# Splitting weights by pairs of k-tiles in the first layer and the attention values, and sharing the split pool with the MLPs

## The chip, the cores and the metric

The kernel runs on one core of one Trainium2 chip. The metric is the time of one execution on the device, in microseconds (us). Engines are named as in the profile: PE multiplies matrices (PEld loads its weights), DVE, ACT and POOL work on vectors, SP issues the DMA transfers from its queue.

## What is computed

Two layers over 256 positions of width 2048, all float32, here in short form. The first is an RWKV-7 time mixing, the second an attention with forget gates over shared keys and values; each is followed by an MLP with squared ReLU of width 8192.

```python
rkv = jnp.einsum('bsnd,nde->bsne', xs[:, :, :3], w_rkv)      # three 2048x2048 projections
y = rwkv7_recurrence(rh, dh, kh, vh, -kk, kk * ah)
x = x + (y * g) @ w_o
x = x + jnp.square(jax.nn.relu(rms_norm(x) @ w_up[0])) @ w_down[0]
k, v, f = split(rms_norm(x) @ w_kvf)                         # keys, values, forget gates
x = x + attention(rms_norm(x) @ fox_w_q, k, v, cumsum(log_sigmoid(f))) @ fox_w_o
x = x + jnp.square(jax.nn.relu(rms_norm(x) @ w_up[1])) @ w_down[1]
out = rms_norm(x)
```

Gains, mixing with the previous position, the low-rank gates and softmax are left out of this extract.

## The kernel before

PE multiplies float32 through operands that are rounded for it (`F32R`). To keep precision every weight is split in two: a high part `wh`, the rounded copy, and a low part `wl`, what the rounding dropped. A product then takes a matmul of the high part with each part of the activations, and one of the low part with their high part. `load_split` does it: a DMA from SP's queue brings a raw tile `wr` (512 KB), ACT casts it to `wh` (L203) and DVE subtracts to get `wl` (L205). A raw tile is free when its last subtraction has ended; a split tile when PE's last matmul with it has.

A raw tile of the first layer holds two k-tiles of 128 rows, 512 columns each. `per` says how many k-tiles go into one split. Before, the first layer (`gemm_steps` for w_rkv and w_o, `gv` for the first layer's values), the attention's keys (`wide_sums` with `per` 1) and its values split one k-tile at a time, 128x512; `narrow_steps`, for the queries and fox_o, takes four k-tiles of 256 columns by twos, 128x512 as well. The MLPs split two k-tiles at once, 128x1024.

The raw tiles of all stages come from the pool `wraw` (4 buffers). The splits outside the MLPs come from `wsp` (5 buffers each of `wh` and `wl`, 128x512), those of the MLPs from a pool `ms` of their own (`WSP`, 4 buffers of 128x1024).

The stages follow one another, with some overlap: the first layer's projections beside the preparation of the recurrence (to about 330 us of the span), the recurrence (to 620), the tail of w_o, the first MLP (660 to 1357), keys and values (to 1540), queries, heads and fox_o (to 1780), and the second MLP. Inside the first layer two plans, written as tables of numbers, mix the streams: `gk`, `gr` and `gv` are the groups of columns of the three projections, `prep` makes the recurrence's operands (kk, bk, ksq and others on DVE; stores to and loads from scratch memory `s_e`, `s_at`, `s_k`, `s_b` through SP). In the second plan every eighth cast goes to DVE (L201) and every fifth subtraction to POOL; these are counted per split. The order on each engine is set by a scheduler that works with estimated times, and each engine and SP's queue take theirs in that order.

Of the kernel before, what the change touches and what calls it, by code (L numbers as in the profile page):

```python
# [18 lines left out]
P = 128  # L19
# [9 lines left out]
RMS_EPS = 1e-6  # L29
CDEC = math.exp(-0.5)  # L30
NEG = -1.0e30
WK, WSP = 2, 4

VEC = ["mix0", "mix1", "ffn0", "ffn1", "fin", "kvn", "xm0", "xm1", "xm2", "xm3", "xm4", "xm5",
       "w0", "a0", "kk", "ka", "rk", "lnw", "lnb"]
# [83 lines left out]
def trunk_kernel(ctx: ExitStack, tc: tile.TileContext, xin, vecs, bfv, c32, c16, w_rkv, w1, w2, a1, a2, g1, g2,  # L119
# [9 lines left out]
    nc.scalar.preload_act_table_set("natural_log_exp_and_others")  # L129

    cpool = ctx.enter_context(tc.tile_pool(name="const", bufs=1))
    wraw = ctx.enter_context(tc.tile_pool(name="wraw", bufs=4))
    wsp = ctx.enter_context(tc.tile_pool(name="wsp", bufs=5))
    big = ctx.enter_context(tc.tile_pool(name="big", bufs=1))
    psm = ctx.enter_context(tc.tile_pool(name="psm", bufs=4, space=PSUM))
    pss = ctx.enter_context(tc.tile_pool(name="pss", bufs=4, space=PSUM))
# [2 lines left out]
    opA = big.tile([P, KT, 2, T], F32R, name="opA")  # L139
# [50 lines left out]

    share = {"n": 0, "h": 0, "l": 0}

    def load_split(src, p, nk, n, per=1, wraw=wraw, wsp=wsp):
        raw = wraw.tile([p, nk, n], F32, tag="wr", name="wr")
        dma(raw, src)
        hl = []
        for k in range(0, nk, per):
            h = wsp.tile([p, per, n], F32R, tag="wh", name="wh")
            c = share["n"] = share["n"] + 1
            if share["h"] and c % share["h"] == 0:  # L200
                V.tensor_copy(h, raw[:, k:k + per, :])  # L201
            else:
                nc.scalar.copy(h, raw[:, k:k + per, :])  # L203
            lo = wsp.tile([p, per, n], F32R, tag="wl", name="wl")
            (G if share["l"] and c % share["l"] == 0 else V).tensor_tensor(  # L205
                lo, raw[:, k:k + per, :], h.bitcast(F32), op=ALU.subtract)
            hl += [(h[:, i, :], lo[:, i, :]) for i in range(per)]
        return hl
# [6 lines left out]
    def gemm_steps(w, col, xh, xl, evac, ks=None, ps=None, ready=None):  # L215
# [6 lines left out]
        if fresh:  # L222
            ps += [psm.tile([P, 2, T], F32, tag="mm", name="mm") for _ in range(2)]
        for k0 in ks[::2]:
            hl = load_split(w[k0 * P:(k0 + 2) * P, col:col + 512].rearrange("(k p) n -> p k n", p=P), P, 2, 512)
            for kk in range(2):
                k = k0 + kk
                assert ready is None or ready(k)
                h, lo = hl[kk]
                for m in range(4):  # L230
                    mm3(ps[m // 2][:, m % 2, :], h[:, m * P:(m + 1) * P], lo[:, m * P:(m + 1) * P],
                        xh[:, k, :], xl[:, k, :], k == ks[0] and fresh, k == KT - 1, m % 2 == 0)
                yield
# [522 lines left out]
    def gv(g):  # L756

        ps = [psm.tile([P, 512], F32, tag="mm", name="mmv") for _ in range(2)]
        for k0 in range(0, KT, 2):
            hl = load_split(w_rkv[2][k0 * P:(k0 + 2) * P, 512 * g:512 * g + 512].rearrange("(k p) n -> p k n", p=P),  # L760
                            P, 2, 512)
            for kk in range(2):
                k, (h, lo) = k0 + kk, hl[kk]
                assert k < mixed[2]
# [196 lines left out]
    def after0(kp):  # L961
        norm2.add(kp)
        operand("kvn", kp, opBH, opBL)
    with tc.tile_pool(name="msp0", bufs=WSP, reuse_waits="tile") as ms, \
            tc.tile_pool(name="mlp0", bufs=2, reuse_waits="tile") as mp:
        for g in range(4):
            gemm_group(w_o, 512 * g, opAH, opAL, o_evac_for(g), range(12, 16), po[g] if g < 2 else None)
        mlp(0, norm, mp, (wraw, ms), opB, opA, after0)


    s_c = dpool.tile([HEADS, T], F32, name="s_c")
# [1 line left out]
    with tc.tile_pool(name="fox", bufs=2, reuse_waits="tile") as fp:  # L973
# [63 lines left out]
        for g in range(4):  # L1037
            ps = [psm.tile([P, 512], F32, tag="mm", name="mmv") for _ in range(2)]
            for k0 in range(0, KT, 2):
                c = D + 512 * g  # L1040
                hl = load_split(w_kvf[k0 * P:(k0 + 2) * P, c:c + 512].rearrange("(k p) n -> p k n", p=P), P, 2, 512)
                for kk in range(2):
                    k = k0 + kk
                    for i in range(2):
# [94 lines left out]

    norm4 = Norm(npool, "n3")  # L1140
    with tc.tile_pool(name="msp1", bufs=WSP, reuse_waits="tile") as ms, \
            tc.tile_pool(name="mlp1", bufs=2, reuse_waits="tile") as mp:

        def after1(kp):
# [2 lines left out]
                return  # L1147
            for k in range(2 * kp if kp < KT // 2 - 1 else 2 * kp - 2, 2 * kp + 2):
                act(xT[:, k, :], xT[:, k, :], AF.Copy, scale=vcol("fin", k))
        mlp(1, norm3, mp, (wraw, ms), opA, opB, after1)  # L1150
        norm4.ln()

        rp = side("rf")[:, 0:T]
# [61 lines left out]
```

## Time and profile before

| | us |
|---|---|
| median of 3 runs | 2475.38 |
| fastest and slowest run | 2474.15, 2476.15 |
| the profiled execution, its time | 2474.56 |
| its span in the trace | 2472.8 |
| PE busy | 2429.4 (98%) |
| DVE busy | 1513.6 (61%) |
| ACT busy | 1235.7 (50%) |
| POOL busy | 243.8 (10%) |

The profiled execution's time is 1.8 us more than its span, which lies around it, and 0.8 us under the median of the runs. Busy shares are means over the span. A line such as `L205 DVE TENSOR_TENSOR wl<-wr,wh 128x512` is the instruction's source line, its engine, operation, written and read tiles, and the shape for one instruction; what follows `|` is the busy time in us, the mean of one in ns, and the engine's idle time ahead of them with what ended it. A time line has the start, the duration and how many instructions stand in the row. Where instructions overlap, the end of one lies behind the start of the next.

### The profile page before, as it was taken

To read this page: it belongs to the slowest core of one execution; us is meant where nothing else is said; L and a number is where in the kernel's file an instruction comes from. 1 tells how busy PE (TensorE), PEld (TensorE's weight loads), DVE (VectorE), ACT (ScalarE), POOL (GpSimd) and SP (SyncE) were. 2 spreads that over 40 slices of the span, in tenths; PEclk is the share of its full clock that TensorE was granted. 3 is DMA by queue.
4 is the path that set the end of the run, shared out by engine and by line. 5 is a ranking of instruction groups with operands and counts; after the bars stand their busy time and mean duration, and the time that the engine had idled before them with its cause. 6 is when DMAs were issued, how large, how long until landed. Compare 5 with 4: busy or idle time off the path is not lost.

```text
span 2472.8 us, 45748 instructions
## 1 busy us (share of the span) xinstructions
PE 2429.4 (98%) x18336; PEld 2087.4 (84%) x18336; DVE 1513.6 (61%) x2201; ACT 1235.7 (50%) x1969; POOL 243.8 (10%) x241
## 2 busy tenths in 40 slices
PE   8999999999999999999999999999999999999998
PEld 6999877689888888888888888888888888888886
DVE  8986666765854455554557565787654555555554
ACT  3766444454654453453455544565454543443543
POOL 2000112221300010000011000111010000000001
PEclk9999999999999999999999999999999999999999
DMA  5777765564766666666665656545656666666653
GB/s 166 229 248 246 261 196 172 185 189 147 230 190 190 194 187 195 190 187 194 191 184 179 189 178 194 170 158 176 201 182 196 190 188 195 190 189 195 189 186 125
DMA packets 276565, 472.56 MB, mean 191 GB/s; under 512 B 23280, under 2 KB 70656, under 8 KB 276352
## 3 DMA queue, kind: packets, MB, share of 16 engines
q1 hardware_dynamic: 276352, 469.64, 61.2%
q8 instruction: 143, 2.34, 0.4%
q14 instruction: 70, 0.57, 0.1%
HBM read 445.44 MB, written 24.13 MB: 190 GB/s over the span
## 4 chain that ended last, share of the span: by engine, by line
PE 91%; DVE 4%; issue 2%; DMA 1%; ACT 1%; POOL 0%; SPq 0%; POOLq 0%; DVEq 0%; ACTq 0%
PE mmw L253 21%; PE mmw L257 11%; PE mmd L390 9%; PE mmd L389 9%; PE mmd L391 9%; PE mmn L271 5%; PE mm L211 3%; PE mm L212 3%; PE mm L213 3%; PE mmn L275 2%; PE mmv L767 1%; PE i L693 1%; PE mmv L768 1%; PE mmv L769 1%; PE zyus L869 1%
## 5 line engine op out<-in xcount | busy, mean ns | idle before, releaser
L205 DVE TENSOR_TENSOR wl<-wr,wh 128x1024 fp32r<-128x1024 f32 (+1 forms) x1001 | 964.1, 974 | 769.2 <-ACT wh L203 682.8
L203 ACT CAST wh<-wr 128x512 fp32r<-128x512 f32 (+1 forms) x1010 | 839.4, 837 | 976.8 <-PE mmd L390 345.0
L253 PE MATMUL mmw<-opB,wh 128*128 128x512 f32 x1280 | 321.2, 393 | 0.0
L253 PEld LDWEIGHTS mmw<-opB,wh 128*128 128x128 f32 x1280 | 230.4, 189 | 41.7 <-ACT nln L351 0.3
L253 PE MATMUL mmw<-opA,wh 128*128 128x512 f32 x1024 | 256.7, 393 | 0.0
L253 PEld LDWEIGHTS mmw<-opA,wh 128*128 128x128 f32 x1024 | 184.4, 189 | 33.3 <-ACT nln L351 0.3
L389 PE MATMUL mmd<-wh,opB 128*128 128x512 f32 x512 | 199.7, 390 | 0.0
L389 PE MATMUL mmd<-wh,opA 128*128 128x512 f32 x512 | 199.7, 390 | 0.0
L390 PE MATMUL mmd<-wh,opA 128*128 128x512 f32 x512 | 199.3, 389 | 0.0
L391 PE MATMUL mmd<-wl,opA 128*128 128x512 f32 x512 | 199.3, 389 | 0.0
L391 PE MATMUL mmd<-wl,opB 128*128 128x512 f32 x512 | 199.3, 389 | 0.0
L390 PE MATMUL mmd<-wh,opB 128*128 128x512 f32 x512 | 199.3, 389 | 0.0
L419 POOL TENSOR_TENSOR ms<-mt 128x512 f32<-128x512 f32 x64 | 78.5, 1239 | 1157.7 <-ACT mt L417 1157.7
L257 PEld LDWEIGHTS mmw<-opB,wl 128*128 128x128 f32 x1280 | 174.5, 190 | 14.9 <-DVE wl L205 2.6
L257 PE MATMUL mmw<-opB,wl 128*128 128x256 f32 x1280 | 178.7, 283 | 1.8 <-DVE wl L205 1.8
L211 PE MATMUL mm<-opA,wh 128*128 128x256 f32 x512 | 150.5, 294 | 0.0
L257 PEld LDWEIGHTS mmw<-opA,wl 128*128 128x128 f32 x1024 | 139.8, 190 | 10.0
L212 PE MATMUL mm<-opA,wh 128*128 128x256 f32 x512 | 145.5, 284 | 0.0
L213 PE MATMUL mm<-opA,wl 128*128 128x256 f32 x512 | 145.1, 283 | 0.0
L257 PE MATMUL mmw<-opA,wl 128*128 128x256 f32 x1024 | 142.8, 282 | 0.0
L391 PEld LDWEIGHTS mmd<-wl,opB 128*128 128x128 f32 x512 | 96.1, 188 | 20.0
L391 PEld LDWEIGHTS mmd<-wl,opA 128*128 128x128 f32 x512 | 96.1, 188 | 20.0
(293 smaller groups left out, 3833.5 us busy)
## 6 DMA issues: line engine op xcount, KB each, us to landing
wr<-in_mlp_w_up_dram SPq DMA_DIRECT2D x256, 512.0 KB, 3.8
wr<-in_mlp_w_down_dram SPq DMA_DIRECT2D x256, 512.0 KB, 3.7
wr<-in_w_rkv_dram SPq DMA_DIRECT2D x96, 512.0 KB, 5.0
wr<-in_w_kvf_dram SPq DMA_DIRECT2D x64, 512.0 KB, 3.7
wr<-in_w_o_dram SPq DMA_DIRECT2D x32, 512.0 KB, 4.6
wr<-in_fox_w_q_dram SPq DMA_DIRECT2D x32, 512.0 KB, 3.5
wr<-in_fox_w_o_dram SPq DMA_DIRECT2D x32, 512.0 KB, 3.7
wr<-in_g_dram SPq DMA_DIRECT2D x8, 512.0 KB, 4.7
```

The source lines that it names most:

```text
L203: nc.scalar.copy(h, raw[:, k:k + per, :])
L205: (G if share["l"] and c % share["l"] == 0 else V).tensor_tensor(lo, raw[:, k:k + per, :], h.bitcast(F32), op=ALU.subtract)
L211: mm(ps, wh, xh, start=first and bank_first, stop=False, skip_group_check=True)
L212: mm(ps, wh, xl, start=False, stop=False, skip_group_check=True)
L213: mm(ps, wl, xh, start=False, stop=last, skip_group_check=True)
L253: mm(ps[m], h[:, m * P:(m + 1) * P], x[:, k].rearrange("p h t -> p (h t)"), start=k == 0, stop=False, skip_group_check=True)
L257: mm(ps[m][:, 0:T], lo[:, m * P:(m + 1) * P], x[:, k, 0, :], start=False, stop=k == KT - 1, skip_group_check=True)
L271: mm(ps[m], hl[i][0][:, m * P:(m + 1) * P], x[:, k0 + i].rearrange("p h t -> p (h t)"), start=k0 + i == 0, stop=False, skip_group_check=True)
L389: mm(ps[i], b[:, k, 0, t], h, start=k == 0, stop=False)
L390: mm(ps[i], b[:, k, 1, t], h, start=False, stop=False)
L391: mm(ps[i], b[:, k, 0, t], lo, start=False, stop=k == KT - 1)
L419: G.tensor_tensor(s, t, t, op=ALU.mult)
```

## The change

The first layer's three projections and w_o, and the attention's values, now call `load_split` with `per` 2: one cast and one subtraction of 128x1024 for two k-tiles. `wsp` holds 3 buffers instead of 5; a buffer there now is as large as its largest tile, a pair. `wraw` holds 3 instead of 4. Keys, queries and fox_o still split 128x512 tiles, through the same 3 buffers. The MLPs get raw tiles of their own (`mr`, 4 buffers) and take their splits in turn from `wsp` and from `ms`, which has 2 buffers (3 + 2 pairs in rotation). Since the counts of `SHARE_B` run per split, the second plan now has half as many splits, and gives DVE 7 casts and POOL 11 subtractions of 128x1024 where it gave 14 and 23 of 128x512.

```diff
@@ -29,7 +29,7 @@
 RMS_EPS = 1e-6
 CDEC = math.exp(-0.5)
 NEG = -1.0e30
-WK, WSP = 2, 4
+WK, WSP = 2, 2
 
 VEC = ["mix0", "mix1", "ffn0", "ffn1", "fin", "kvn", "xm0", "xm1", "xm2", "xm3", "xm4", "xm5",
        "w0", "a0", "kk", "ka", "rk", "lnw", "lnb"]
@@ -129,8 +129,8 @@
     nc.scalar.preload_act_table_set("natural_log_exp_and_others")
 
     cpool = ctx.enter_context(tc.tile_pool(name="const", bufs=1))
-    wraw = ctx.enter_context(tc.tile_pool(name="wraw", bufs=4))
-    wsp = ctx.enter_context(tc.tile_pool(name="wsp", bufs=5))
+    wraw = ctx.enter_context(tc.tile_pool(name="wraw", bufs=3))
+    wsp = ctx.enter_context(tc.tile_pool(name="wsp", bufs=3))
     big = ctx.enter_context(tc.tile_pool(name="big", bufs=1))
     psm = ctx.enter_context(tc.tile_pool(name="psm", bufs=4, space=PSUM))
     pss = ctx.enter_context(tc.tile_pool(name="pss", bufs=4, space=PSUM))
@@ -190,6 +190,15 @@
 
     share = {"n": 0, "h": 0, "l": 0}
 
+    class Turns:
+
+        def __init__(self, *pools):
+            self.pools, self.n = pools, {}
+
+        def tile(self, shape, dtype, tag, name):
+            n = self.n[tag] = self.n.get(tag, -1) + 1
+            return self.pools[n % len(self.pools)].tile(shape, dtype, tag=tag, name=name)
+
     def load_split(src, p, nk, n, per=1, wraw=wraw, wsp=wsp):
         raw = wraw.tile([p, nk, n], F32, tag="wr", name="wr")
         dma(raw, src)
@@ -222,7 +231,7 @@
         if fresh:
             ps += [psm.tile([P, 2, T], F32, tag="mm", name="mm") for _ in range(2)]
         for k0 in ks[::2]:
-            hl = load_split(w[k0 * P:(k0 + 2) * P, col:col + 512].rearrange("(k p) n -> p k n", p=P), P, 2, 512)
+            hl = load_split(w[k0 * P:(k0 + 2) * P, col:col + 512].rearrange("(k p) n -> p k n", p=P), P, 2, 512, 2)
             for kk in range(2):
                 k = k0 + kk
                 assert ready is None or ready(k)
@@ -758,7 +767,7 @@
         ps = [psm.tile([P, 512], F32, tag="mm", name="mmv") for _ in range(2)]
         for k0 in range(0, KT, 2):
             hl = load_split(w_rkv[2][k0 * P:(k0 + 2) * P, 512 * g:512 * g + 512].rearrange("(k p) n -> p k n", p=P),
-                            P, 2, 512)
+                            P, 2, 512, 2)
             for kk in range(2):
                 k, (h, lo) = k0 + kk, hl[kk]
                 assert k < mixed[2]
@@ -962,10 +971,11 @@
         norm2.add(kp)
         operand("kvn", kp, opBH, opBL)
     with tc.tile_pool(name="msp0", bufs=WSP, reuse_waits="tile") as ms, \
+            tc.tile_pool(name="mraw0", bufs=4, reuse_waits="tile") as mr, \
             tc.tile_pool(name="mlp0", bufs=2, reuse_waits="tile") as mp:
         for g in range(4):
             gemm_group(w_o, 512 * g, opAH, opAL, o_evac_for(g), range(12, 16), po[g] if g < 2 else None)
-        mlp(0, norm, mp, (wraw, ms), opB, opA, after0)
+        mlp(0, norm, mp, (mr, Turns(wsp, ms, wsp, ms, wsp)), opB, opA, after0)
 
 
     s_c = dpool.tile([HEADS, T], F32, name="s_c")
@@ -1038,7 +1048,7 @@
             ps = [psm.tile([P, 512], F32, tag="mm", name="mmv") for _ in range(2)]
             for k0 in range(0, KT, 2):
                 c = D + 512 * g
-                hl = load_split(w_kvf[k0 * P:(k0 + 2) * P, c:c + 512].rearrange("(k p) n -> p k n", p=P), P, 2, 512)
+                hl = load_split(w_kvf[k0 * P:(k0 + 2) * P, c:c + 512].rearrange("(k p) n -> p k n", p=P), P, 2, 512, 2)
                 for kk in range(2):
                     k = k0 + kk
                     for i in range(2):
@@ -1139,6 +1149,7 @@
 
     norm4 = Norm(npool, "n3")
     with tc.tile_pool(name="msp1", bufs=WSP, reuse_waits="tile") as ms, \
+            tc.tile_pool(name="mraw1", bufs=4, reuse_waits="tile") as mr, \
             tc.tile_pool(name="mlp1", bufs=2, reuse_waits="tile") as mp:
 
         def after1(kp):
@@ -1147,7 +1158,7 @@
                 return
             for k in range(2 * kp if kp < KT // 2 - 1 else 2 * kp - 2, 2 * kp + 2):
                 act(xT[:, k, :], xT[:, k, :], AF.Copy, scale=vcol("fin", k))
-        mlp(1, norm3, mp, (wraw, ms), opA, opB, after1)
+        mlp(1, norm3, mp, (mr, Turns(wsp, ms, wsp, ms, wsp)), opA, opB, after1)
         norm4.ln()
 
         rp = side("rf")[:, 0:T]
```

The changed file's lines stand 9 lower behind `Turns` (L205 is L214, L213 is L222) and 10 lower behind the first MLP (L1131 is L1141).

On DVE in the first layer, from the last subtractions of the first group of keys' weights on, the rows before (`xs` are mixed activations, `hsl`, `ksq` and `kkk` belong to `prep`, `kr` evacuates the first product):

```order
L205 TENSOR_TENSOR wl<-wr,wh 128x512
L525 SCALAR_TENSOR_TENSOR xs<-xT,vec,hT 128x256 x3
L368 TENSOR_TENSOR opB<-xs,opB 128x256
L525 SCALAR_TENSOR_TENSOR xs<-xT,vec,hT 128x256 x3
L179 COPY kr<-mm 128x512
L525 SCALAR_TENSOR_TENSOR xs<-xT,vec,hT 128x256 x5
L205 TENSOR_TENSOR wl<-wr,wh 128x512
L525 SCALAR_TENSOR_TENSOR xs<-xT,vec,hT 128x256 x5
L182 TENSOR_TENSOR hsl<-ksq,hsh 128x512
L525 SCALAR_TENSOR_TENSOR xs<-xT,vec,hT 128x256 x3
L633 TENSOR_SCALAR ksq<-kss 128x512
L205 TENSOR_TENSOR wl<-wr,wh 128x512 x3
```

The rows there now:

```order
L534 SCALAR_TENSOR_TENSOR xs<-xT,vec,hT 128x256 x3
L377 TENSOR_TENSOR opB<-xs,opB 128x256
L534 SCALAR_TENSOR_TENSOR xs<-xT,vec,hT 128x256 x2
L179 COPY kr<-mm 128x512
L534 SCALAR_TENSOR_TENSOR xs<-xT,vec,hT 128x256 x5
L182 TENSOR_TENSOR hsl<-ksq,hsh 128x512
L534 SCALAR_TENSOR_TENSOR xs<-xT,vec,hT 128x256 x3
L642 TENSOR_SCALAR ksq<-kss 128x512
L534 SCALAR_TENSOR_TENSOR xs<-xT,vec,hT 128x256 x6
L182 TENSOR_TENSOR kkk<-kkk,ksq 128x512
L214 TENSOR_TENSOR wl<-wr,wh 128x1024
```

The four subtractions, of which one stood between two rows of `xs` and three ahead of `kkk`, have become two pairs behind `kkk`.

On SP's queue, in the second unit of `prep`, before (the three loads of the first row are loads 16 to 18 of w_rkv, counted from 0; `s_e`, `s_at`, `s_k` and `s_b` are scratch):

```order
L195 DMA wr<-in_w_rkv_dram 128x2x512 x3
L622 DMA w_1128<-in_w_dram 96x512
L622 DMA a_1130<-in_a_dram 96x512
L698 DMA AT<-s_at 128x512
L700 DMA Bi<-s_b 128x512
L654 DMA s_e_103<-ke 128x512
L667 DMA s_at<-ksq 128x512
L661 DMA s_k_102<-kk_743 128x512
L700 DMA Ki<-s_k 128x512
L672 DMA s_b<-bk 128x512
L672 DMA s_k<-bk 128x512
L195 DMA wr<-in_w_rkv_dram 128x2x512 x4
```

And now, from load 17 (the first row with `wr`) and 18 (the second) on:

```order
L204 DMA wr<-in_w_rkv_dram 128x2x512
L707 DMA AT<-s_at 128x512
L663 DMA s_e_103<-ke 128x512
L676 DMA s_at<-ksq 128x512
L670 DMA s_k_102<-kk_711 128x512
L709 DMA Bi<-s_b 128x512
L204 DMA wr<-in_w_rkv_dram 128x2x512
L681 DMA s_b<-bk 128x512
L681 DMA s_k<-bk 128x512
L204 DMA wr<-in_w_rkv_dram 128x2x512 x3
```

Load 17 now stands behind the two small loads of the next unit, and load 18 behind the reload of `Bi` and the stores from `ke`, `ksq` and `kk`, directly ahead of the two stores of `bk`.

On DVE at the end of the heads, where fox_o's first groups end (L1131, now L1141, adds the product to the stream `xT`; L363, now L372, makes the low part of the second MLP's operand), before:

```order
L205 TENSOR_TENSOR wl<-wr,wh 128x512
L1131 TENSOR_TENSOR xT<-mmn,xT 128x256 x5
L363 SCALAR_TENSOR_TENSOR opA<-xT,vec,opA 128x256
L1131 TENSOR_TENSOR xT<-mmn,xT 128x256
L363 SCALAR_TENSOR_TENSOR opA<-xT,vec,opA 128x256
L1131 TENSOR_TENSOR xT<-mmn,xT 128x256
L205 TENSOR_TENSOR wl<-wr,wh 128x512
L1131 TENSOR_TENSOR xT<-mmn,xT 128x256
L363 SCALAR_TENSOR_TENSOR opA<-xT,vec,opA 128x256
L205 TENSOR_TENSOR wl<-wr,wh 128x512 x2
L363 SCALAR_TENSOR_TENSOR opA<-xT,vec,opA 128x256
L205 TENSOR_TENSOR wl<-wr,wh 128x512 x7
```

And now:

```order
L214 TENSOR_TENSOR wl<-wr,wh 128x512
L1141 TENSOR_TENSOR xT<-mmn,xT 128x256 x5
L372 SCALAR_TENSOR_TENSOR opA<-xT,vec,opA 128x256
L1141 TENSOR_TENSOR xT<-mmn,xT 128x256
L372 SCALAR_TENSOR_TENSOR opA<-xT,vec,opA 128x256
L1141 TENSOR_TENSOR xT<-mmn,xT 128x256
L372 SCALAR_TENSOR_TENSOR opA<-xT,vec,opA 128x256
L1141 TENSOR_TENSOR xT<-mmn,xT 128x256
L214 TENSOR_TENSOR wl<-wr,wh 128x512 x2
L372 SCALAR_TENSOR_TENSOR opA<-xT,vec,opA 128x256
L214 TENSOR_TENSOR wl<-wr,wh 128x512 x3
L214 TENSOR_TENSOR wl<-wr,wh 128x1024
```

The subtraction that stood between the last rows of `xT` has moved behind all of them and one more of `opA`, and subtractions of 128x1024, the first of the second MLP, stand among those of fox_o.

## The prediction

> **What bounds the kernel now.** I read the page first (busy shares and the chain that ended last), then a table of busy times by stage, then what PE waited for, and last the time lines of the places where PE waits for a split.
>
> ```profile
> PE 2429.4 (98%) x18336; PEld 2087.4 (84%) x18336; DVE 1513.6 (61%) x2201; ACT 1235.7 (50%) x1969; POOL 243.8 (10%) x241
> PE 91%; DVE 4%; issue 2%; DMA 1%; ACT 1%; POOL 0%; SPq 0%; POOLq 0%; DVEq 0%; ACTq 0%
> ```
>
> PE holds 91% of the chain; 4% of 2472.8 us, about 99 us, runs through DVE, where the change acts. The next rows say where (us; PE, PEld, DVE, ACT and POOL busy with counts; granted clock; DMA share; GB/s).
>
> ```profile
> 14.00:130.00 116.00, 107.63 (x715) 95.48 (x716) 108.33 (x220) 72.26 (x154) 12.63 (x16) 0.97 0.59 189
> 130.00:330.00 200.00, 196.24 (x2273) 179.46 (x2271) 143.69 (x247) 121.02 (x231) 14.92 (x15) 1.00 0.77 252
> 330.00:620.00 290.00, 276.64 (x5730) 230.00 (x5731) 184.91 (x356) 128.88 (x272) 64.62 (x72) 0.96 0.56 173
> 620.00:660.00 40.00, 38.22 (x278) 35.65 (x277) 36.58 (x44) 25.39 (x44) 17.11 (x11) 1.00 0.67 216
> 660.00:1357.00 697.00, 697.00 (x3543) 595.20 (x3543) 387.70 (x407) 334.17 (x422) 47.66 (x37) 1.00 0.63 192
> 1357.00:1540.00 183.00, 182.92 (x929) 153.83 (x928) 106.67 (x177) 92.85 (x165) 7.09 (x8) 1.00 0.61 184
> 1540.00:1680.00 140.00, 139.40 (x812) 120.90 (x811) 106.17 (x266) 81.24 (x193) 14.86 (x26) 1.00 0.50 159
> ```
>
> Only two stretches have DVE as full as PE: 14 to 130 (108.33 of 116 us) and 620 to 660 (36.58 of 40). In the first MLP PE is busy for 697.00 of 697.00 us and in keys and values for 182.92 of 183, so a cheaper split is worth nothing there. From 130 to 330 PE lacks 3.8 us; from 330 to 620 it lacks 13.4, in the recurrence, whose waits are not for weights.
>
> **The change, part by part.** *Cheaper splits.* Two casts and two subtractions of 128x512 become one each of 128x1024. The groups by shape (busy us, mean ns, then idle before):
>
> ```profile
> L203 ACT CAST wh<-wr 128x1024 fp32r<-128x1024 f32 x512 | 534.9, 1049 | 672.6 <-PE mmd L390 345.0 <-PE mmw L253 272.3 <-issue 39.2
> L203 ACT CAST wh<-wr 128x512 fp32r<-128x512 f32 x498 | 304.8, 619 | 304.2 <-PE mm L212 68.6 <-PE mmn L271 58.1 <-PE mmv L768 48.3
> L205 DVE TENSOR_TENSOR wl<-wr,wh 128x1024 fp32r<-128x1024 f32 x512 | 626.1, 1228 | 582.7 <-ACT wh L203 580.3
> L205 DVE TENSOR_TENSOR wl<-wr,wh 128x512 fp32r<-128x512 f32 x489 | 338.2, 709 | 186.5 <-ACT wh L203 102.6 <-PE mmw L257 37.6 <-PE mmn L275 34.0
> L205 POOL TENSOR_TENSOR wl<-wr,wh 128x512 fp32r<-128x512 f32 x23 | 30.7, 1337 | 72.6 <-ACT wh L203 50.2 <-PE mm L213 7.4 <-PE i L693 6.5
> ```
>
> A pair saves 2 x 709 - 1228 = 190 ns by durations, but durations overlap where DVE runs back to back, so the saving of a full DVE is read from runs of subtractions, six single ones and two pairs:
>
> ```profile
> 91.83 3.70 DVE L205 TENSOR_TENSOR wl<-wr,wh 128x512 fp32r<-128x512 f32 x6
> 676.32 2.36 DVE L205 TENSOR_TENSOR wl<-wr,wh 128x1024 fp32r<-128x1024 f32 x2 [0.26 <-ACT wh L203]
> ```
>
> Start to start a single takes (3.70 - 0.71) / 5 = 0.60 us, a pair 2.36 - 1.23 = 1.13. The saving is 1.20 - 1.13 = 0.07 us a load. In the groups of 14 to 130 alone this row counts the loads:
>
> ```profile
> L205 DVE TENSOR_TENSOR wl<-wr,wh 128x512 fp32r<-128x512 f32 x49 | 32.9, 694 | 4.2 <-ACT wh L203 4.2
> ```
>
> 49 subtractions are about 25 loads: 25 x 0.07 = -1.8 us, with ends 0 (PE waits for something else there) and 25 x 0.19 = -4.8. I take -1.8, since DVE is 93% full there and its pitch, not its duration, counts. The tail of w_o (620 to 660) has 13 singles, about 7 loads: -0.5, ends 0 and -1.3. The other loads of w_rkv and w_o, and all of V, save on DVE and ACT beside a full PE: 0; the cover is the idle DVE time of the table (56 of 200 us from 130 to 330), and without it they would gain 0.07 each. Of the sums on POOL, 23 of 1.34 us become 11 of twice the size: the weights of that stage wait several us for PE, 0 either way.
>
> *Later first parts.* A pair's first low half is ready after 1.05 + 1.23 = 2.28 us instead of 0.62 + 0.71 = 1.33, so 0.95 later where PE waits for it. That is at load 8 of w_rkv above all, where the order on DVE also puts the pair behind kkk:
>
> ```profile
> 58.95 0.68 DVE L205 TENSOR_TENSOR wl<-wr,wh 128x512 fp32r<-128x512 f32 x1
> 63.42 0.68 DVE L633 TENSOR_SCALAR ksq<-kss 128x512 f32<-128x512 f32 x1
> 64.03 1.88 DVE L205 TENSOR_TENSOR wl<-wr,wh 128x512 fp32r<-128x512 f32 x3
> 65.83 0.69 DVE L182 TENSOR_TENSOR kkk<-kkk,ksq 128x512 f32<-128x512 f32 x1
> ```
> ```profile
> 63.95 0.47 PE L213 MATMUL mm<-opB,wl 128*128 128x256 f32 x1
> ```
>
> PE uses the first low part at 63.95. Moved behind kkk, with ksq and kkk earlier by the 2.4 us of four subtractions at 0.60 that no longer stand ahead of them (kkk from 65.83 to about 64), the pair starts near 64.6 and ends near 65.8: PE waits 1.6 to 1.9 us more. Part returns, since kkk and what follows are earlier. From 65 to 330 PE waits for wl only twice:
>
> ```profile
> PE mm L213 <- DVE wl L205: 1.5, 2, 0.8
> ```
>
> Load 8 and these two give 1.6 + 2 x 0.95 = 3.5 at most, 0 if DVE's lead grows; I take +1.8, nearest to load 8 alone.
>
> *Three raw buffers for four.* A load is issued when the subtraction three loads before has ended, not four. A load lands 5.0 us after its issue:
>
> ```profile
> wr<-in_w_rkv_dram SPq DMA_DIRECT2D x96, 512.0 KB, 5.0
> ```
>
> In a stretch where PE sets the pace the chain goes through its matmuls at 0.12 us each:
>
> ```profile
> 121.66 0.12 PE mm L211
> ```
>
> A load is 24 of them, 2.88 us; three loads 8.64. The loop is landing 5.0 + cast 1.05 + subtraction 1.23 + about 0.1 = 7.4, so it fits with 1.2 us to spare. It is tight where DVE gives the subtractions in bursts:
>
> ```profile
> 78.93 4.44 SPq L195 DMA_DIRECT2D wr<-in_w_rkv_dram  x3
> ...
> 92.38 0.32 SPq L672 DMA_DIRECT2D s_k<-bk  x1
> 92.80 4.08 SPq L195 DMA_DIRECT2D wr<-in_w_rkv_dram  x4
> ```
> ```profile
> 98.50 0.62 ACT L203 CAST wh<-wr 128x512 fp32r<-128x512 f32 x1 [0.98 <-DMA wr<-in_w_rkv_dram]
> ```
> ```profile
> 100.73 0.50 PE L599 MATMUL kss<-hsh,onesr 128*128 128x512 f32 x1
> ```
>
> The third load of the 78.93 row (load 18) will wait for load 15, whose second subtraction is now the first of the six at 91.83. As a pair it goes, by the order on DVE, ahead of the two products bk that stand before it now, and ends near 91.83 - 3 x 0.60 + 1.23 = 91.3. Load 18 then lands near 96.5 and is split near 99. PE has loads 15 to 17 until kss at 100.73, so it doesn't wait for load 18. Behind it on SP stand the two stores of bk (the second is the 92.38 row), which can't come before bk, near 92. The load after it goes out near 93.7 instead of 92.80: 0.9 late on a piece of the chain (92.80, 5.60 us DMA, below). DVE waits for load 18 where it went on before, up to 3.6 us. I take +1.0, ends 0 and 3.6.
>
> *Three split buffers in keys, queries and fox_o.* Their tiles stay 128x512, so the split runs three tiles ahead instead of five.
>
> ```profile
> ACT wh L203 <- PE mmw L253: 45.3, 55, 5.7
> ```
>
> In keys ACT already waits for a free buffer; the remaining lead of two tiles, 2.8 us of PE, covers 1.33 of split: 0. At fox_o's first groups it doesn't, since DVE then adds to xT:
>
> ```profile
> 1678.66 0.69 DVE L205 TENSOR_TENSOR wl<-wr,wh 128x512 fp32r<-128x512 f32 x1 [1.29 <-PE mmn L275]
> 1679.27 1.82 DVE L1131 TENSOR_TENSOR xT<-mmn,xT 128x256 f32<-128x256 f32 x5
> 1682.60 0.69 DVE L205 TENSOR_TENSOR wl<-wr,wh 128x512 fp32r<-128x512 f32 x1
> ```
> ```profile
> 1682.42 1.12 PE L275 MATMUL mmn<-opB,wl 128*128 128x256 f32 x8
> ```
>
> The low parts that PE uses at 1682.42 will be those of DVE's next subtraction behind the burst. It starts near 1683.3, one operand row later than the 1682.60 here, and ends near 1684.0: +1.6, ends 0 and 3 (a second tile late too).
>
> *MLPs.* Five pairs for four and raw buffers of their own: PE is full there, 0.
>
> **Sum**: -1.8 - 0.5 + 1.8 + 1.0 + 1.6 = +2.1 us on the profiled 2474.56, 2476.7. The median of the runs, 2475.38, is 0.8 higher, so the forecast is 2477. The ends together: -4.8 - 1.3 = -6.1, and 3.5 + 3.6 + 3.0 = +10.1. About 5 us (0.2%) is what a measurement can tell here, so this is no change.
>
> **Rivals.** *DVE's relief passes through (faster).* If all of 14 to 130 hangs on DVE with its durations, the gain is 4.8 + 1.3 = 6.1 and the three delays disappear into the lead that the larger split pool (three pairs hold six tiles, five before) gives: 2469. For it: DVE 93% full. Against: the pitch of 0.60. Chance 0.22.
>
> *Three raw buffers starve the first layer (slower).* It decides once landing exceeds 5.0 + 1.2 = 6.2 us. One piece of the chain shows 5.60, so the margin isn't far. With landing 0.5 above it, each of some 25 loads from 130 to 210 loses 0.5 / 3: +4.2, with the sum above 2481. Chance 0.16.
>
> *Coarser splits come too late (slower).* If not three but eight places have PE just behind the split, they lose 8 x 0.95 = 7.6 instead of 1.8: 2483. Against it: PE's waits for wl are 1.5 us from 65 to 330. Chance 0.12. The Trainium skill, "Perfetto Trace Analysis", section "Optimizing Scalar/DVE Operations", says that larger operations help where the engine is saturated and that breaking them up lets work finish sooner where it isn't but causes bubbles elsewhere. By that rule, the first stretch gains and the others lose; no run here has shown the loss yet.
>
> *Half-clock periods come or go.* The chain's issue gaps on PE are each followed by a period at half clock:
>
> ```profile
> 92.80 5.60 DMA wr<-in_w_rkv_dram
> ...
> 328.53 2.83 issue
> ...
> 470.87 1.86 issue
> ```
> ```profile
> 332.00:342.60 10.60, 10.60 (x184) 7.99 (x179) 3.93 (x8) 3.39 (x8) 2.31 (x2) 0.52 0.54 176
> ```
> ```profile
> 472.00:479.00 7.00, 6.27 (x82) 4.73 (x81) 4.66 (x9) 1.72 (x3) 2.29 (x4) 0.52 0.41 121
> ```
>
> A period costs 0.48 of its length: 5.1 us at 332, 3.4 at 472. PE's program there hardly changes but the DMA traffic beside it does; one fewer gives 2472 to 2473, one more 2480 to 2482. Chance 0.06 each way. The Trainium skill, "TensorE: Matmul & The Clock Gate", Part 1, asks for an idle window of about 3.4 us before the clock halves; here gaps of 1.86 and 2.83 us stand ahead of it, so the trace doesn't bear the figure out.
>
> **How the numbers follow.** The forecast has 0.38, the relief 0.22, starving 0.16, late splits 0.12, the clock 0.12. Faster by over 5 us: the relief without its near half (0.17) and a low end of the others, 0.24. Slower: half of starving and most of late splits, one clock period, and the sum's own upper end, 0.27. Within: 0.49. The range runs from the relief with one clock period fewer (2467) to late splits with a raw delay above (2486).
>
> **What would show it.** Right: 128x1024 subtractions from 14 to 130 at a pitch near 1.13 and DVE busy about 1.8 us less; L222, which was L213, waiting near 64 to 66; load 19 of w_rkv issued near 93 to 94; a wait of mmn for wl near 1682. Wrong: PE waiting for wl at many places from 65 to 330 (late splits), casts waiting for DMA in every load from 130 to 210 (starving), PE's start of the first MLP 5 us earlier (relief), or another count of stretches at clock 0.5.

## The result, and the profile after

The changed kernel takes 2492.77 us (median of 4 runs, 2491.57 to 2499.51), the kernel before 2475.77 on the same chip: 1.0075 of its time, 95% interval 1.0062 to 1.0088, or some 17 us more. The forecast was no change, and the time lies 7 us above the range (2467 to 2486). The profiled execution after took 2491.57 us with a span of 2489.8; against the span before, 2472.8, that is 17.0 us.

The busy line and the chain's shares by engine, from the page of after:

```profile
PE 2434.4 (98%) x18336; PEld 2091.4 (84%) x18336; DVE 1494.7 (60%) x2045; ACT 1212.7 (49%) x1816; POOL 247.0 (10%) x230
PE 85%; DVE 3%; DMA 3%; issue 2%; ACT 2%; POOL 0%; SPq 0%; POOLq 0%; ACTq 0%; DVEq 0%
```

DVE is busy for 18.9 us less, as the change meant. But PE's share of the chain fell from 91% to 85%, and transfers rose from 1% to 3%: PE waits for data that come late. The table by stage, with the columns of the one before:

```profile
14.00:130.00 116.00, 106.18 (x710) 95.21 (x711) 107.10 (x197) 69.30 (x128) 15.22 (x16) 0.96 0.58 185
130.00:330.00 200.00, 191.47 (x1966) 176.00 (x1965) 129.47 (x185) 110.05 (x173) 14.70 (x12) 0.99 0.73 239
330.00:620.00 290.00, 271.77 (x5864) 223.19 (x5863) 178.96 (x316) 119.97 (x233) 62.56 (x63) 0.96 0.55 171
660.00:1357.00 697.00, 695.67 (x3550) 593.87 (x3550) 390.72 (x400) 335.79 (x420) 55.02 (x42) 1.00 0.63 192
```

PE now lacks 8.5 us from 130 to 330, where it lacked 3.8, and 18.2 from 330 to 620, where it lacked 13.4. The share of full clock from 330 to 620 is 0.96 as before.

Windows fixed in time mix different work when one kernel lags. So I matched the n-th matmul of each source line in two traces. This table has the start in a kernel minus the start in the kernel before, in us, as a median over the matmuls that began in the 20 us from each time in the kernel before. Each row comes from one profiled execution; the kernels beside `after` are the experiments below.

```
              60   100   200   280   320   500   600   700  1380  1600  1700
after        2.0   0.6   3.2   6.0  11.1   9.8  15.3  15.1  15.5  15.7  17.0
e2           0.5   2.8   3.2   8.7   9.8  15.3  15.6  17.3  17.3  17.5  17.1
e5           1.0  -1.4  -1.6  -1.8   0.4  -0.5   6.5   5.8   6.1   6.3   7.8
e9           0.9  -1.4  -1.6  -1.6  -0.4  -4.3   1.2   0.4   0.8   1.2   2.6
e13          1.8   0.6   1.9   4.6   7.4   2.7   9.5   9.1   9.5   9.7  12.1
e17          1.8   2.7   4.6   3.6   5.6   5.0  12.6  12.7  13.1  13.6  15.1
e18          0.2   0.9   1.2   0.2   0.4  -4.4  -2.8  -2.8  -2.8  -2.8  -2.9
```

The changed kernel loses 15 of its 17 us before 620, in the first layer's weights and the recurrence, changes little over the MLP and the keys (15.1 at 700, 15.5 at 1380) and loses 1.3 at fox_o (15.7 at 1600, 17.0 at 1700).

What ACT waited for from 130 to 330 (us in total, times, longest), in the kernel before, then in after:

```profile
ACT wh L203 <- DMA wr<-in_w_rkv_dram: 15.7, 7, 5.0
```
```profile
ACT wh L212 <- DMA wr<-in_w_rkv_dram: 51.4, 20, 10.1
```

Seven casts waited for their weights, now twenty. From 230 to 330 a landed tile lay 6.5 us (mean; median 3.5) before its cast began, and lies 1.7 (0.55) now; a landing took 5.4 us and takes 5.3. Transfers didn't slow down; the reserve of landed weights is gone. The chain of after where the lag grows, start, duration, what:

```profile
250.50 1.75 PE mmg L593 x8
252.24 0.02 issue
252.26 4.43 DMA wr<-in_w_rkv_dram
...
296.36 2.35 DVE wl L214
298.72 0.38 SPq L204
299.15 0.46 SPq L709
299.67 6.33 DMA k<-s_k
306.07 2.18 POOL k L182
...
310.29 6.56 DMA wr<-in_w_rkv_dram
```

The first row is the one that I had not thought of: `mmg` are the matmuls of the output gate. Their weights g2 come in four tiles of 512 KB from the same raw pool, and no split frees them, only PE's last matmul with them. A weight load starts 0.02 us behind it. So it isn't true of every raw tile, as I wrote ahead of the prediction, that it is free with its last subtraction. How the gate tiles (L586) and the weight loads (L204) take turns on SP's queue, and PE's last matmuls with the first two gate tiles:

```profile
220.87 0.38 SPq L586 DMA_DIRECT2D wr<-in_g_dram  x1
...
226.26 0.39 SPq L204 DMA_DIRECT2D wr<-in_w_rkv_dram  x1
...
232.75 0.38 SPq L204 DMA_DIRECT2D wr<-in_w_rkv_dram  x1
...
234.72 0.43 SPq L586 DMA_DIRECT2D wr<-in_g_dram  x1
238.95 0.38 SPq L204 DMA_DIRECT2D wr<-in_w_rkv_dram  x1
```
```profile
228.15 2.00 PE L593 MATMUL mmg<-gh,wr 128*128 128x256 f32 x8
239.91 2.00 PE L593 MATMUL mmg<-gh,wr 128*128 128x256 f32 x8
```

The four gate tiles are held, from issue to last matmul, from 211.89 to 230.1, 220.87 to 241.9, 234.72 to 252.2 and 246.48 to 262.3. They overlap: for 50 us one of the three raw buffers is theirs, and for 22 us of these two are. From 226.26 to 238.95 the weight loads go out one at a time, 6.2 to 6.5 us apart; the buffer that comes free in between, at 230.1, goes to the next gate tile at 234.72.

The later rows of the chain show the first layer's end: a load late in SP's queue, behind it a reload of `k` from scratch, and behind the stores that follow a load that lands only after 6.56 us.

### The profile page after: what moved, and what is told of

The parts are those of the page before. It is cut to its first block, busy times and chain, and to the rows that moved or that the text cites. A ratio compares the mean times of both kernels' runs of the same rounds, so it can differ in the third digit from the quotient of the medians.

```text
span 2489.8 us, 45249 instructions
## 1 busy us (share of the span) xinstructions
PE 2434.4 (98%) x18336; PEld 2091.4 (84%) x18336; DVE 1494.7 (60%) x2045; ACT 1212.7 (49%) x1816; POOL 247.0 (10%) x230
## 4 chain that ended last, share of the span: by engine, by line
PE 85%; DVE 3%; DMA 3%; issue 2%; ACT 2%; POOL 0%; SPq 0%; POOLq 0%; ACTq 0%; DVEq 0%
PE mmw L262 21%; PE mmw L266 11%; PE mmd L398 9%; PE mmd L399 9%; PE mmd L400 9%; PE mmn L280 5%; PE mmn L284 2%; PE mm L220 2%; PE mm L222 2%; PE mm L221 2%; DMA wr<-in_w_rkv_dram 2%; PE zyus L878 1%; PE i L702 1%; DVE wl L214 1%; PE mmv L1056 1%
## 5 line engine op out<-in xcount | busy, mean ns | idle before, releaser
L214 DVE TENSOR_TENSOR wl<-wr,wh 128x1024 fp32r<-128x1024 f32 (+1 forms) x852 | 936.0, 1109 | 770.6 <-ACT wh L212 700.1
L212 ACT CAST wh<-wr 128x1024 fp32r<-128x1024 f32 (+1 forms) x857 | 813.2, 954 | 952.1 <-PE mmd L399 347.4
L222 PE MATMUL mm<-opA,wl 128*128 128x256 f32 x512 | 145.4, 284 | 1.4 <-DVE wl L214 1.3
```

Source lines behind the costliest of these rows:

```text
L222: mm(ps, wl, xh, start=False, stop=last, skip_group_check=True)
```

## The experiments

The theory at the start, A in the expectations, was *raw buffers*: three for four cost the time. Its rivals: *pairs* (a coarse split is late wherever PE is close behind it), *SP's queue* (loads now stand behind stores and reloads that wait), and later *POOL* (its 12 pairs are too long). All ratios are to the kernel before on the same chip.

### One part alone: e1 and e2

e1 is the kernel before with pairs everywhere and four raw buffers; its split buffers are 3 of high and 2 of low pairs, since no more fit.

```diff
-    wsp = ctx.enter_context(tc.tile_pool(name="wsp", bufs=5))
+    wsp = ctx.enter_context(tc.tile_pool(name="wsp", bufs=3))   # wl: bufs=2
-            hl = load_split(... P, 2, 512)         # gemm_steps, gv, values
+            hl = load_split(... P, 2, 512, 2)
-            hl = load_split(... P, 4, 256, 2)      # narrow_steps
+            hl = load_split(... P, 4, 256, 4)
-            ps = wide_sums(w_kvf, 512 * g, opB, (wraw, wsp), 1)
+            ps = wide_sums(w_kvf, 512 * g, opB, (wraw, wsp))
```

> The kernel before with pairs in the first layer and the values, but four raw buffers as before: in the same memory the split pool has three pairs for the high and two for the low parts. The MLPs are as before. Keys, queries and fox_o split by pairs too. Theory A (three raw buffers starve the first layer): without that loss only the start (about 1 us) is left, and fox_o's wait goes, so 2474 to 2478, and casts wait for weights' DMA from 130 to 330 about as long as before (16 us). Theory B (the pairs themselves come too late or too coarsely): most of the loss stays, 2486 to 2493.

Measured: 2500.09 us, 1.0094 [1.0071, 1.0117], outside what either theory expected, and by the intervals no faster than the changed kernel. The time decides nothing, because the two low buffers are a fault of their own. What PE and DVE waited for from 620 to 670, the two rows that name each other:

```profile
PE mm L214 <- DVE wl L206: 6.1, 3, 3.5
DVE wl L206 <- PE mm L214: 9.1, 5, 3.7
```

DVE waits for PE to free a low part and PE for DVE to make the next. The waits of ACT in e1 do speak for raw buffers: from 130 to 330 casts wait 17.9 us in 9 times for their weights, near the kernel before (15.7) and far from the changed one (51.4).

e2 is the kernel before with three raw buffers and nothing else:

```diff
-    wraw = ctx.enter_context(tc.tile_pool(name="wraw", bufs=4))
+    wraw = ctx.enter_context(tc.tile_pool(name="wraw", bufs=3))
```

> The kernel before, only with three raw buffers for four, everywhere, its splits still 128x512. Theory A: a loss of 8 to 14 us up to the first MLP (2484 to 2490), with casts that wait for the weights' DMA 40 us and more from 130 to 330. Theory B: within 3 us of before up to the first MLP.

Measured: 2489.98 us, 1.0047 [1.0029, 1.0066], or 11.6 us (7.2 to 16.3). The median lies above that, for two of the six runs took 2481.6 and 2483.6 us and the other four 2488.9 to 2491.7; the profile (lag 17.1 at 1700) is of one of the four. The same row of waits, 130 to 330, in e2:

```profile
ACT wh L203 <- DMA wr<-in_w_rkv_dram: 39.8, 19, 6.4
```

Without any pair, nineteen casts wait. The missing buffer alone does that.

### SP's queue: e3, e14, e15, e16

e3 moves the scratch stores and reloads of the changed kernel to POOL's queue, e14 its weight loads of the first layer:

```diff
-    ldma = nc.sync.dma_start          # e3
-    sdma = nc.sync.dma_start
+    ldma = nc.gpsimd.dma_start
+    sdma = nc.gpsimd.dma_start
-        dma(raw, src)                 # e14, up to the first MLP
+        nc.gpsimd.dma_start(raw, src)
```

> The changed kernel, with the scratch stores and reloads issued from POOL's queue, so that on SP's queue a weight load no longer stands behind a reload that waits. Theory A in its form that the waits on SP's queue empty the three raw buffers: casts wait for weights' DMA less than half as long as now from 240 to 330 (27 us now), and the time falls by 4 to 10 us, unless POOL's own work holds the reloads up. If the count of buffers alone does it: within 3 us of the changed kernel's 2492.

> The changed kernel with the first layer's weight loads issued from POOL's queue instead of SP's, where they stand behind stores and reloads; three raw buffers as before. POOL has little of its own up to 300 us. If the wait in SP's queue (a mean of 3.5 us from a free buffer to the issue, from 230 to 330) is what makes three buffers too few: casts wait for weights' DMA under 25 us from 130 to 330 (51 now) and the drift against before at 300 us is below 4 us (9.6 now). If three buffers are too few even with prompt issue: 7 us or more at 300.

Measured: 2504.99 us, 1.0118 [1.0097, 1.0139], and 2505.26 us, 1.0123 [1.0106, 1.0140]; both are slower than the changed kernel. e3 falls back by 16 us between 280 and 320 (lags 8.3 and 24.2), where a reload stands on the chain:

```profile
303.76 10.02 DMA r<-s_r
```

In e14 ACT still waits for weights, and POOL, where the loads are issued now, for the subtraction that frees a raw tile (130 to 330):

```profile
POOL wr L205 <- DVE wl L215: 107.6, 35, 12.3
ACT wh L213 <- DMA wr<-in_w_rkv_dram: 60.2, 24, 4.8
```

The chain of e14 shows the loop of one raw tile by itself:

```profile
232.58 1.24 DVE wl L215
233.81 0.29 issue
234.10 4.39 DMA wr<-in_w_rkv_dram
...
238.57 1.05 ACT wh L213
239.62 0.02 issue
239.65 1.24 DVE wl L215
```

Subtraction to subtraction that is 7.07 us. A queue without stores ahead of the loads didn't cure the waits, so their place behind SP's stores doesn't look like the main cause (the control follows); what it adds around 300 us isn't separated, since POOL's queue brings delays of its own.

e15 and e16 make the same move in the kernel before and in e12 (below):

> The kernel before with the first layer's weight loads on POOL's queue. A control, and a version that might be faster: 2470 to 2476 if SP's queue costs it anything up to 330 us; 2476 to 2484 if POOL's own waits in the recurrence hold the loads up.

> Pairs with four raw buffers, nothing of the splits on POOL and no casts on DVE in the second plan, and the first layer's weight loads on POOL's queue. If the recurrence's late reloads of b and k came from loads ahead of them on SP's queue, the 2 us lost there at 540 to 560 go, and with the gain of the pairs up to 300 us: 2470 to 2475. If POOL's waits hold the loads up: 2476 to 2484.

Measured: 2484.53 us, 1.0036 [1.0020, 1.0051], and 2484.76 us, 1.0041 [1.0026, 1.0055]. With four raw buffers, POOL's queue costs about 9 us in both (e16 against e12). So on POOL's queue the changed kernel stands 0.87% above the kernel before (e14 against e15), on SP's 0.75%: the loss is about the same on either queue. e15 has a wait on POOL's subtraction at 290 to 330, and e16 loses at the start, 0 to 100, where PE waits for `xs`:

```profile
PE mmv L770 <- POOL wl L206: 6.8, 1, 6.8
```
```profile
PE lps L560 <- DVE xs L536: 7.8, 3, 6.9
```

### The changed kernel with four raw buffers: e5, control e6

e5 gives the changed kernel its fourth raw buffer. To make room the MLPs use `wraw` again, and some other pools lose a buffer; e6 takes the same buffers from the kernel before.

```diff
-    wraw = ctx.enter_context(tc.tile_pool(name="wraw", bufs=3))
+    wraw = ctx.enter_context(tc.tile_pool(name="wraw", bufs=4))
-    negv = cpool.tile([P, 2 * KT], F32, name="negv")
+    negv = vec[:, VIX["w0"] * KT:VIX["w0"] * KT + 2 * KT]
-    ... kr bufs=4, csb bufs=3, qT bufs=5, mr bufs=4
+    ... kr bufs=3, csb bufs=2, qT bufs=4, wraw for mr
```

> The changed kernel (pairs, three split buffers of a pair each) with its fourth raw buffer back; the MLPs take their raw tiles from it. The memory comes from one buffer fewer for the keys' products (kr, 3 for 4) and, in the attention, for csb and qT. Theory A (the lost raw buffer is the cause): most of the 15 us lost up to the first MLP returns, 2475 to 2481 in all, and casts wait for the weights' DMA about 16 us from 130 to 330 instead of 51. Theory B (pairs cost as much by themselves): 2486 to 2493.

> A control for the previous one: the kernel before with the same three buffers fewer (kr 3, csb 2, qT 4) and nothing else. If these don't matter: 2473 to 2479. If kr does: slower up to 330 us of the span, and the previous kernel is to be read against this one.

Measured: e5 2482.14 us, 1.0026 [1.0014, 1.0038]; e6 2474.52 us, 0.9996 [0.9983, 1.0008]. The room costs nothing, and the fourth buffer returns 0.49% (by the intervals 0.31 to 0.67) of the 0.75%, 12.1 us, as much as e2 lost. ACT's row in e5:

```profile
ACT wh L213 <- DMA wr<-in_w_rkv_dram: 5.8, 4, 1.9
```

A landed tile lies 7.9 us (median 4.7) before its cast from 230 to 330, more than before the change. With the buffer back, DVE's relief shows: e5's lag goes from +1.2 at 20 us to -1.8 at 280, e9's from 1.1 to -1.6, and that of the control e6 from 1.6 to 1.5.

### The gate's tiles: e8, e17, control e18

e8 gives the gate's weights a raw buffer of their own (256 columns, 2 KB per partition):

```diff
-            raw = wraw.tile([P, 2, 512], F32, tag="wr", name="wr")
-            dma(raw, g2[:, 512 * g:512 * g + 512].rearrange(...))
...
+                raw = pp.tile([P, 2, 256], F32, tag="graw", name="graw")
+                dma(raw, g2[:, 512 * g + 256 * b:512 * g + 256 * b + 256].rearrange(...))
```

> The changed kernel with the gate's weights (four tiles of 512 KB that take turns in the raw pool until PE's mmg has used them) in a buffer of their own, by halves of 256 KB, and kr 3 for 4. Theory A in the form that these tiles take one of only three raw buffers from 219 to 260: the 2.8 us lost near 260 go, and casts wait less for weights there; about 2489 to 2490. If they don't matter: 2492 to 2493.

Measured: 2495.92 us, 1.0082 [1.0061, 1.0104], no better. The chain says why: the one small buffer became the bound.

```profile
236.44 3.26 DMA graw<-in_g_dram
239.74 2.01 PE mmg L593 x8
241.77 3.59 DMA graw<-in_g_dram
```

e17 therefore loads the first 256 columns of g2 once and uses them for every group, so that the gate neither takes a raw tile nor waits for one; e18 does it in the kernel before. The other columns and 3.5 of the gate's four loads are left out, so there are fewer transfers as well as fewer raw tiles taken; these two are not told apart.

```diff
+            if g == 0:
+                raw = pp.tile([P, 2, 256], F32, tag="graw", name="graw")
+                dma(raw, g2[:, 0:256].rearrange("(k p) n -> p k n", p=P))
```

> The changed kernel with three raw buffers for the weights alone: the gate's weights are loaded once, a half tile of 256 KB in a buffer of its own, and used for all eight of mmg's products, so three and a half of the gate's four loads are left out (kr 3 for 4 makes room). If the gate's tiles in the raw pool are what makes three buffers too few near 220 to 270: the drift against the kernel before grows by less than 1 us from 220 to 280 (2.8 us in the changed kernel), and the time is 2488 to 2490. If three are too few for the projections' loads alone, the drift there is as before and only what follows differs: 2491 to 2494.

> The control: the kernel before with the gate's weights loaded once in the same way, four raw buffers. If the gate's tiles cost nothing there: 2474 to 2478, and the drift from 220 to 280 is within 0.5 us.

Measured: e17 2487.96 us, 1.0051 [1.0034, 1.0067]; e18 2474.62 us, 0.9999 [0.9989, 1.0008]. With four raw buffers the gate's tiles cost nothing; with three they cost 0.24% (by the intervals 0.03 to 0.45), about 6 us, half of the missing buffer's price by this middle value. From 220 to 330, in e17 (in after 29.7 us in 8 times):

```profile
ACT wh L212 <- DMA wr<-in_w_rkv_dram: 2.7, 1, 2.7
```

e17's lag falls by 1.0 from 200 to 280, as much as e18's does; the changed kernel's grows by 2.8. Against the control that places 2.8 us by 280, and 6.1 by 320 (grown by 7.9 in after and by 1.0 in e17, fallen by 0.8 in e18). Later e17 loses much of this again, mostly from 500 to 600, and in the single profiles the two kernels end only 1.9 apart (17.0 and 15.1 at 1700); that 6 us are left at the end rests on the timed ratio alone.

### POOL's share: e9, e10, e12, e13

These set the counts of `SHARE_B`: no subtraction on POOL in e5 (e9), in the kernel before (e10) and in the changed one (e13); in e12, e5 without casts on DVE either.

```diff
-SHARE_B = {"h": 8, "l": 5}
+SHARE_B = {"h": 8, "l": 0}
```

> The changed kernel with four raw buffers (as in the run before with kr 3), and in the second plan no subtraction on POOL: all pairs are subtracted on DVE. There the pairs lose about 6 us between 500 and 600 us of the span, where a POOL pair of 2.4 us holds a raw tile, a weight load stands on SP's queue until it is free, and the reloads of b and k behind it come late for PE's g2a. If that is it, 3 to 5 us of the 6 return: 2476 to 2479. If the recurrence's loss has another cause: 2481 to 2484.

> A control: the kernel before with no subtraction on POOL in the second plan. If POOL's share matters little with 128x512 splits: 2473 to 2479. If it is POOL in itself that delays the recurrence: 2 to 4 us faster than before.

> As the first of these, with no cast on DVE in the second plan either. If DVE's casts of pairs (0.95 us each, 7 of them) delay the recurrence's DVE work: 1 to 3 us faster than the first. If not: within 1 us.

> The changed kernel (three raw buffers) without subtractions on POOL in the second plan. With four raw buffers the same edit gave 5 to 6 us. If the two losses add: 2486 to 2488. If with three buffers the weights are late anyhow, so that POOL doesn't matter: 2491 to 2494.

Measured: e9 2476.27 us, 1.0004 [0.9995, 1.0013]; e10 2479.09, 1.0011 [0.9999, 1.0023]; e12 2477.67, 1.0006 [0.9993, 1.0019]; e13 2488.42, 1.0053 [1.0038, 1.0068]. POOL's pairs cost 0.22% both with four raw buffers (e5 to e9, 0.07 to 0.37) and with three (after to e13, 0.02 to 0.42): 5.4 us, beside the raw buffers' 12. Before, POOL's single subtractions cost nothing (e10 is no faster without them). Their groups on POOL in after, 12 and not the 11 that I had counted, to lay beside the 1337 ns of before:

```profile
L214 POOL TENSOR_TENSOR wl<-wr,wh 128x1024 fp32r<-128x1024 f32 x12 | 29.0, 2413 | 71.1 <-ACT wh L212 58.1 <-DVE wh L210 12.9
```

Where the 5.4 us arise is only partly settled. I expected a wait for the reload of `b` near 548; in e9 it is still there. One place is visible, 505 to 545: with a subtraction of 2.4 us on POOL there (517.81 in e5, 528.19 in after) PE stops in the recurrence for what the profile can't name, in after and in e5:

```profile
PE i L702 <- issue: 1.2, 1, 1.2
```
```profile
PE i L703 <- issue: 1.6, 2, 0.8
```

e9 and e13 have no such row, and their lags stay level from 510 to 530, while those of e5 and after grow by 2.0 and 2.6. The casts on DVE make no difference (e12 against e9). The rest is spread from 340 to 520, mixed with half-clock stretches that come and go.

### Finer steps: e4, e7, e11

e4 splits keys by two and queries and fox_o by four in the changed kernel, e7 gives the kernel before five raw and four split buffers, e11 splits the first load of e9 singly:

```diff
-            hl = load_split(... P, 4, 256, 2)                  # e4
+            hl = load_split(... P, 4, 256, 4)
-wraw bufs=4, wsp bufs=5                                         # e7
+wraw bufs=5, wsp bufs=4
-            hl = load_split(... P, 2, 512, 2)                  # e11
+            hl = load_split(... P, 2, 512, 1 if share["n"] < 2 else 2)
```

> The changed kernel with keys, queries and fox_o split by pairs as well, so that three buffers hold six tiles there. If the wait at fox_o's first groups comes from the lead of only three tiles of 128x512, the 1.5 us lost there and the 0.4 in keys go: about 2 us faster than the changed kernel (2490 to 2491). If it comes from the order on DVE alone, it stays: within 0.5 us.

> The kernel before with its memory moved the other way: five raw buffers for four, and four split buffers of 128x512 for five. If raw buffers still limit the first layer with four of them: 3 to 8 us faster there (2467 to 2472). If four are enough: 2474 to 2478, with a small loss at fox_o for the split buffer.

> As the first of these, and the very first weight load split by single k-tiles. PE's first low part was 1.2 us late with the pair; if that is lost for good, this is 1 us faster than the first of these; if it is made up for by 100 us of the span (the drift against before is back there), no difference within 0.5 us up to 130 us.

Measured: e4 2497.24 us, 1.0080 [1.0055, 1.0105], no faster than the changed kernel; e7 2484.96, 1.0034 [1.0022, 1.0046], slower than either guess; e11 2479.92, 1.0015 [1.0002, 1.0027]. At fox_o (1660 to 1720) PE's wait becomes one for another tile in e4, and shrinks with one split buffer more in e7:

```profile
PE mmn L280 <- DVE opB L377: 1.4, 1, 1.4
```
```profile
PE mmn L275 <- DVE wl L205: 0.3, 1, 0.3
```

A fifth raw buffer bought nothing in the first layer (lag +2.0 at 320); by the lag e7 loses 3.4 us from 500 to 600 and 3.6 around 640, with one split buffer less. e11 removes the 1.2 us at the start and keeps that up to 200 (-2.8 against -1.6), but is no faster in total. None of the kernels beats the one before by more than its interval.

## Why the prediction failed

**The step that failed most: three raw buffers for four.** Forecast +1.0, ends 0 and 3.6; measured about 12 (11.6 in e2, 12.1 from e5 to after). The loop of one tile was right: 7.4 forecast, 7.07 in e14's chain. The number of tiles in it was wrong. I counted 3 x 2.88 = 8.64 us as if all three served the projections. While a gate tile holds one, two are left: 2 x 2.88 = 5.76, less than the loop; while two gate tiles overlap, one is left: 2.88. That is about half of the price by e17's middle value. The other half I read as bursts, which a mean loop doesn't see: the fourth buffer's landed tile was the reserve against a late issue or a landing like the 6.56 us above, over the 6.2 from which I let three buffers starve. The vanished reserve is measured (median 3.5 to 0.55 us); that it makes up the whole other half is not shown. The low-rank products `lps` take raw tiles that only PE frees, too (four from 103.20 to 138.1 in after); no run here leaves these out, so their part isn't known. The rival of starving, at 0.16 and 4.2 us, had the right outcome, casts that wait for their weights, but for another reason: landings did not grow beyond 6.2 us, they stayed at 5.3 on average. Its place held only a small part of it (the lag grows by 2.6 us from 100 to 200), and its size was a third.

**The second: POOL's subtractions.** Forecast 0 either way, since the weights there wait for PE; measured +5.4 (e9, e13). One subtraction took 1.8 times as long (2413 ns for 1337), and the cover was read from the weights alone, not from what else stands in that stage.

**Right in sign, and within its ends: cheaper splits.** -1.8 forecast, ends 0 and -4.8. With four raw buffers the lag falls by 3.0 us from 20 to 280 (e5). The pairs in after's first stretch, and two back to back:

```profile
L214 DVE TENSOR_TENSOR wl<-wr,wh 128x1024 fp32r<-128x1024 f32 x24 | 29.0, 1218 | 2.6 <-ACT wh L212 2.6
```
```profile
91.89 2.35 DVE L214 TENSOR_TENSOR wl<-wr,wh 128x1024 fp32r<-128x1024 f32 x2
```

The pitch is 2.35 - 1.22 = 1.13, as forecast; DVE is busy 1.23 us less (108.33 to 107.10), where I had looked for 1.8. The tail of w_o, -0.5 forecast, gave -0.2 in after (600 to 700 in the table) and -0.7 in e5.

**Later first parts: the place was right, the size by luck, and it didn't last.** PE's L222 waits for load 8 for 0.90 us, half of the 1.8 forecast. The lag of +2.0 at 60 looks like the forecast only because it holds the lateness of the first load of all, 1.2 us as a pair, which was missed (the lag is +1.4 at 20). At 80 it is 0.1.

```profile
66.36 0.39 PE L222 MATMUL mm<-opB,wl 128*128 128x256 f32 x1 [0.90 <-DVE wl L214]
```

**Load 19** was issued at 93.13, forecast 93 to 94, so the reading of SP's order was right, and the cost was elsewhere:

```profile
93.13 5.44 SPq L204 DMA_DIRECT2D wr<-in_w_rkv_dram  x3
```

**fox_o: right.** +1.6 forecast; 1.48 us at the place named:

```profile
1699.22 1.35 PE L284 MATMUL mmn<-opB,wl 128*128 128x256 f32 x8 [1.48 <-DVE wl L214]
```

**MLPs 0, keys 0, values 0:** measured 0.0, +0.4 and +0.2 by the lag.

**The rivals.** Relief was real but small beside the losses. Late splits were not it: from 130 to 330 PE waits for low parts for 1.3 us. Half-clock periods took a small part at most: what the granted clock leaves out from 14 to 620 is, by the two tables by stage, 4.6 + 2.0 + 11.6 = 18.2 us (0.04, 0.01 and 0.04 of the stages) against 3.5 + 0 + 11.6 = 15.1 before, about 3 us more of the 17. Whether these periods follow from the waits isn't shown.

By the rule of the Trainium skill ("Perfetto Trace Analysis", "Optimizing Scalar/DVE Operations") larger operations help a saturated engine, and breaking operations up helps where an unsaturated one causes bubbles. The runs agree with the first for DVE (-3.0 us in e5). The second they show at the first load alone, where splitting singly starts PE 1.2 us earlier (e11), though not in the total. The rule speaks of Scalar and Vector; on POOL, pairs cost 5.4 us and single subtractions nothing.

The sum by the runs: 12.1 (after to e5), 5.4 (e5 to e9) and e9's rest of +1.0 (relief against the start, fox_o and keys; -1.2 to 3.2 by its interval) give 18.5, against 17.0 by medians and 18.6 by the ratio. These three are steps of one path from the changed kernel to the one before, so they add up to the ratio by construction. What checks them is that the parts come out alike elsewhere: 11.6 us for the raw buffer in the kernel before (e2), 5.4 for POOL with three raw buffers (e13).

## What to carry to other kernels

Before a buffer is traded for larger operations, list everything that takes tiles from that pool, and how long each holds one: a rare tenant that is freed late takes a whole buffer out of the loop, and two that overlap take two. Read the reserve (landed to used), not only the mean loop: here a median of 3.5 us of it went with the fourth buffer. And when operations are grouped, shares that are counted per operation move whole groups to the slow engine: set them anew.

## What the hardware showed unexpectedly

A DMA issue of a first-layer weight load takes POOL 0.72 us, where SP takes 0.38 (medians of 96 loads in e14 and in after); e14's time line of POOL, and after's of SP:

```profile
234.10 0.72 POOL L205 DMA_DIRECT2D wr<-in_w_rkv_dram x1 [12.31 <-DVE wl L215]
```
```profile
90.79 0.38 SPq L204 DMA_DIRECT2D wr<-in_w_rkv_dram  x1
```

The half-clock stretch of before at 332 to 342.6 (0.52) is absent in e18, whose work there is the same but for the gate:

```profile
332.00:342.60 10.60, 8.93 (x267) 6.75 (x269) 5.15 (x11) 4.55 (x11) 2.57 (x3) 1.00 0.58 198
```

e18's lag falls by 4 us there, while its median time equals that of before. So a lag inside the recurrence, from one profile, is good to about 4 us, and only the timed ratios carry the sizes above.
